# One decode step of a hybrid layer: small stores and skewed loads issued by POOL instead of SP, and copies of old cache rows placed behind weight loads

## The chip, the cores and the metric

The kernel runs on one core of one Trainium2 chip. The metric is the device time of one execution in microseconds; every kernel is run several times and the median is taken. TensorE is called PE in the profile, VectorE DVE, ScalarE ACT, GpSimd POOL and SyncE SP. SP computes nothing here: it only issues transfers, in order. POOL does both, it computes and issues, also in order.

## The reference, cut to what matters

One step of a layer for two groups of tokens with the same weights: 512 prompt tokens of one sequence and 64 sample tokens (8 sequences of 8), with a width of 1024. The input is scaled and shifted by a vector that depends on the sequence, then projected once; two branches (chunkwise retention with 4 heads, and dilated window attention in 3 groups with a relative bias) are gated, added and projected, and a second block gathers rows of an expert table.

```python
def _ada(c, w_ada, b_ada):
    mod = jax.nn.silu(c) @ w_ada + b_ada
    return jnp.split(mod[:, None, :], 6, axis=-1)
...
    def step(s, inp):
        qc, kc, vc = inp
        scores = jnp.einsum('bihd,bjhd->bhij', qc, kc) * intra
        o = jnp.einsum('bhij,bjhe->bihe', scores, vc)
        o = o + jnp.einsum('bihd,bhde->bihe', qc, s) * q_dec
        s = s * chunk_dec + jnp.einsum('bjhd,bjhe->bhde', kc * k_dec, vc)
        return s, o
```

Part of the output are the new retention states of both groups and the new caches of the attention. For the sample group a new cache is the old one without its oldest rows and with the 8 new ones, so most of it is a copy of old rows from one place in HBM to another.

## The kernel before

**Weights.** All weights stream through in units of 128 x 1024 numbers (512 KB), in a fixed order. `load_units` (L392) has SP load a unit into one of 3 raw buffers (`wraw`; 4 more serve in the first part of the kernel). ACT makes the upper half of its digits (`whi`, L315), DVE the rest (`wlo`, L316), and PE multiplies three times (`mm3`, L423 to L425). Later units that feed the experts are split by ACT (L1433) and POOL (L1434). SP issues a load when the raw buffer is free, that is, when `wlo` of the unit three earlier is done.

**What else SP issues.** Besides the weights nearly everything: constants, rows of old caches, outputs. The places of this change are five:
- L491: `ada_half` works out a quarter of a modulation vector (`m`), PE spreads it over 9 rows, and the 9 x 256 result (`m9`, one buffer) is stored into `modD` in HBM. 16 times, from 247 to 582 us.
- L525: the bias vectors of the attention are made in pieces (`vt`, two buffers) and stored into `vecD` in HBM. 6 times.
- L531: `skewed` loads `vecD` once and writes it many times, one row for each query position, into another tensor in HBM: `skp` 1024 rows for the prompt, `sks` 64 rows for the sample. 3 of each. What reads them later (L650, L1213) stays on SP.
- L711: `retention_s` stores the new state of a sample head, 128 x 8 x 128 numbers. 4 times.
- L936: `retention` stores the new state of a prompt head (`st`), 128 x 128 numbers. 4 times.

**Copies of old rows.** `copy_old(n, ins)` takes the next n of 104 copies and has SP issue them behind the instruction `ins`:

```python
    def copy_old(n, ins):
        with tc.issue_after(ins):
            for _ in range(n):
                p = next(old, None)
                if p:
                    SP.dma_start(*p)
```

`CR = 8` of them come with each head of `retention`, 32 in all; the others come with weight loads later on and stay where they are. `CS_ = 0`, so the call at L711 issues none.

**What POOL does.** At the start it scales and shifts the transposed input of both groups (`xT`, L508 and L509, two halves). From 64 to 433 us it loads the cached keys of the sample group (`kt`, L742, 32 tiles of 588 KB, 128 rows) and finishes each tile by copying the new keys into it (L744), for which it waits until the tile has landed. Later it gathers the rows of the experts (L1111).

**What sets the order.** A scheduler sorts the instructions of each engine by a simulated timeline, and each engine then runs its list in order. So a change of the issuing engine, or of what `copy_old` is tied to, moves other rows too.

Of the kernel before, what the change touches and what calls it, by code (L numbers as in the profile page):

```python
# [29 lines left out]
NVEC = VEC_G[3]  # L30
# [29 lines left out]
CR = 8  # L60
CS_ = 0
# [163 lines left out]
def body(tc, I, O, dbg=None):  # L225
    nc = tc.nc
    PE, DVE, ACT, POOL, SP = nc.tensor, nc.vector, nc.scalar, nc.gpsimd, nc.sync
# [3 lines left out]
    def raw(ap, offset, dims):  # L231
        return bass.AP(tensor=ap.tensor, offset=ap.offset + offset, ap=dims)
# [62 lines left out]
# [6 lines that stand above are left out]
# [69 lines left out]
    raws, units, state = [], [], {"done": 0, "bank": ac_ps, "ada": None}  # L370
# [38 lines left out]
    def take(name, c, u, n=2):  # L409

        a = state["done"]
        while len(units) < len(order) and sum(not plain(i) for i in range(a, len(units))) < UB:
            load_units()
            if len(units) == len(raws):
                break
            split_unit()
        load_units()
        assert order[a:a + n] == [(name, c, u + i) for i in range(n)] and len(units) >= a + n, (order[a], name, c, u)
        state["done"] += n
        return units[a:a + n]  # L420
# [42 lines left out]
    modD = DR.tile([9, 4096], F32, name="modD")  # L463
    xT = A.tile([128, 8, NS + L], F32, name="xT")

    def ada_half(pl, c, half):

        w = take("w_ada", c, 2 * half)
        ps = sp_ps()
        for z in range(2):  # L470
            for q in range(4):
                PE.matmul(ps[32 * q:32 * q + 32, 0:256], cst[:, 4 * z + q, :], *both(w, 4 * z + q), start=z == 0, stop=z == 1)
        m = pl.tile([106, 256], F32, name="m19", tag="m19", bufs=3)
        o = 512 * c + 256 * half
        SP.dma_start(m[105:106, :], I["b_ada"][:, o:o + 256])
        ACT.activation(m[0:105, :], ps[0:105, 0:256], AF.Copy)
        pt = tr_ps()
        if c < 4:
            for b in range(2):
                PE.matmul(pt[:, 128 * b:128 * b + 65], m[:, 128 * b:128 * b + 128], sel19[:, 0:65], start=True, stop=True)  # L480
            v = pt[:, 0:256].rearrange("p (b c) -> p b c", b=2)[:, :, 0:65]
            b = 4 * (c % 2) + 2 * half
            if c < 2:
                DVE.tensor_copy(shT[:, b:b + 2, :], v)
            else:
                DVE.tensor_scalar(scT[:, b:b + 2, :], v, 1.0, None, op0=OP.add)
        else:
            PE.matmul(pt[0:9, 0:256], sel19[:, 65:74], m, start=True, stop=True)
            t = pl.tile([9, 256], F32, name="m9", tag="m9", bufs=1)
            DVE.tensor_copy(t, pt[0:9, 0:256])  # L490
            SP.dma_start(modD[:, o - 2048:o - 1792], t)  # L491

    hh, hl = wide("xh"), wide("xl")
    h = lambda k, s=slice(None): (hh[:, k, s], hl[:, k, s])
# [18 lines left out]
    vecD = DR.tile([8, NVEC], F32, name="vecD")  # L513
# [4 lines left out]
    for g in range(NG):  # L518
        for o in range(VEC_G[g], VEC_G[g + 1], 512):
            e = min(o + 512, VEC_G[g + 1])  # L520
            ps = ac_ps()
            PE.matmul(ps[0:8, :e - o], rel[:, 8 * g:8 * g + 8], oh[:, o:e], start=True, stop=True)
            t = A.tile([8, 512], F32, name="vt", tag="vt", bufs=2)
            DVE.tensor_copy(t[:, :e - o], ps[0:8, :e - o])
            SP.dma_start(vecD[:, o:e], t[:, :e - o])  # L525
    A.release()

    def skewed(name, off, n, rows):

        t = DR.tile([8, rows, n], F32, name=name)  # L530
        SP.dma_start(t, raw(vecD, off, [[NVEC, 8], [0, rows], [1, n]]))  # L531
        return lambda h0, h, r, first, w, step=1: raw(t, h0 * rows * n + first, [[n - step, r], [rows * n, h], [1, w]])

    def skewed_p(g):
# [133 lines left out]
    def retention_s(hp):  # L668
        qks = RS.tile([64, 512], F32, name="qks", tag="qks", bufs=1)
        for half in range(2):  # L670
            proj_s(RS, qks[:, 256 * half:256 * half + 256], hs, take("w_rqk_s", hp, 2 * half))
        q4 = qks.rearrange("p (n m z d) -> p n m z d", n=2, m=2, z=2)
        rs4 = rope_s.rearrange("p i n (z d) -> p i n z d", z=2)
        for n in range(2):
            for z in range(2):
                DVE.tensor_tensor(r1[:, n, :, z], q4[:, n, :, z], rs4[:, 0, n, z, None, :].to_broadcast([64, 2, 64]), op=OP.mult)
                POOL.tensor_tensor(r2[:, n, :, z], q4[:, n, :, 1 - z], rs4[:, 1, n, z, None, :].to_broadcast([64, 2, 64]), op=OP.mult)
        DVE.tensor_tensor(r1, r1, r2, op=OP.add)
        rot = r1.rearrange("p n m z d -> p (n m z d)")
        qkT = RS.tile([128, 4, 64], F32, name="qkT", tag="qkT", bufs=1)  # L680
        transpose64(qkT, rot, 4)
        ons = sp_ps()
        for j in range(2):
            hd = 2 * hp + j
            hcol = slice(128 * hd, 128 * hd + 128)
            diag = raw(qm, 0, [list(qm.ap[0]), [NB * TS + TS, NB], [1, TS]])
            bt = lambda a: a.rearrange("p (b t) -> p b t", b=NB)
            DVE.tensor_tensor(diag, bt(qkT[:, j, :]), bt(qdec_s[:, hd, :]), op=OP.mult)
            psc = tr_ps()
            PE.matmul(psc[0:64, 0:64], qkT[:, 2 + j, :], qkT[:, j, :], start=True, stop=True)  # L690
            sc = RS.tile([64, 64], F32, name="scs", tag="scs", bufs=2)
            DVE.tensor_tensor(sc, psc[0:64, 0:64], intra_s[:, hd, :], op=OP.mult)
            s0 = RS.tile([128, NB, 128], F32, name="s0", tag="s0", bufs=2)
            with tc.issue_after(state["load"]):
                SP.dma_start(s0, I["state"][hd])
            vb = vbs[j]
            o = ons[0:64, 128 * j:128 * j + 128]
            PE.matmul(o, sc, rvs[:, hcol], start=True, stop=False)
            for b in range(NB):
                PE.matmul(o, qm[:, b].rearrange("p b t -> p (b t)"), s0[:, b, :], start=False, stop=b == NB - 1)  # L700
            POOL.tensor_tensor(vb, rvs[:, None, hcol].to_broadcast([64, NB, 128]),
                               bmask[:, :, None].to_broadcast([64, NB, 128]), op=OP.mult)
            kds = RS.tile([64, 128], F32, name="kds", tag="kds", bufs=2)
            DVE.tensor_scalar(kds, rot[:, 256 + 128 * j:384 + 128 * j], kdec_s[:, hd:hd + 1], None, op0=OP.mult)
            dec = float(np.exp(np.float32(LG[hd] * np.float32(TS))))
            for q in range(2):
                pn = tr_ps()
                PE.matmul(pn, kds, vb[:, 4 * q:4 * q + 4, :], start=True, stop=True)
                s4 = s0[:, 4 * q:4 * q + 4, :]
                DVE.scalar_tensor_tensor(s4, s4, dec, pn.rearrange("p (b e) -> p b e", b=4), op0=OP.mult, op1=OP.add)  # L710
            copy_old(CS_, SP.dma_start(O["st_s"][0, :, hd].rearrange("b d e -> d b e"), s0).ins)  # L711
        y = head_norm(RS, ons[0:64, 0:256].rearrange("p (c e) -> p c e", c=2), 2)
        DVE.tensor_tensor(y[:, 0:2, :], y[:, 0:2, :], rgs[:, 256 * hp:256 * hp + 256].rearrange("p (c e) -> p c e", c=2), op=OP.mult)
        pt = tr_ps()
        for j in range(2):
            PE.transpose(pt[:, 64 * j:64 * j + 64], y[:, j, :], ident[0:64, 0:64])
        stack64(ras[:, 2 * hp:2 * hp + 2, :], pt[:, 0:128].rearrange("p (j t) -> p j t", j=2))
# [192 lines left out]
    def retention(hp):  # L910
        for j in range(2):
            hd = 2 * hp + j
# [18 lines left out]
            st = R.tile([128, 4, 128], F32, name="st", tag="st", bufs=2)  # L931
            dec = float(np.exp(np.float32(LG[hd] * np.float32(128))))
            DVE.tensor_copy(st[:, 0, :], pst[:, 0:128])
            for c in range(1, 4):
                DVE.scalar_tensor_tensor(st[:, c, :], st[:, c - 1, :], dec, pst[:, 128 * c:128 * c + 128], op0=OP.mult, op1=OP.add)
            copy_old(CR, SP.dma_start(O["st_p"][0, 0, hd], st[:, 3, :]).ins)  # L936
            po = ac_ps()
            for c in range(4):
                s = slice(128 * c, 128 * c + 128)
# [25 lines left out]
    G2, t = s4k("G2s"), s4k("l1s")  # L965
# [4 lines left out]
    B2, t = s4k("B2s"), s4k("l1bs")  # L970
# [183 lines left out]
    t = T.tile([8, 4, 128], F32, name="sel8", tag="st8", bufs=2)  # L1154
# [46 lines left out]
    for g in range(NG):  # L1201
# [8 lines left out]
        for hf in range(2):  # L1210
            n = 256 if g == 0 else 128
# [83 lines left out]
    for z, s in enumerate((NM[0], LS[0])):  # L1295
# [3 lines left out]
        t = T.tile([8, 512], F32, name="st8", tag="st8", bufs=2)  # L1299
# [28 lines left out]
    for p in range(4):  # L1328
        for g in range(NG):
# [5 lines left out]
            else:  # L1335
                t = T.tile([128, 512], F32, name="mt", tag="lg", bufs=LGB)
# [55 lines left out]
    for c, ts in ((0, (0, 1, 2, 3)), (1, (0, 1, 2, 3)), (2, (0,)), (3, (0,)), (2, (1,)), (3, (1,)), (2, (2, 3)), (3, (2, 3))):  # L1392
# [6 lines left out]
        for t in ts:  # L1399
# [13 lines left out]
            for kq in range(2):  # L1413
# [4 lines left out]
                o = (slice(None), slice(0, 4), tiles[t])  # L1418
# [237 lines left out]
```

## Time and profile before

| | |
|---|---|
| median of 3 runs | 2457.9 us (2453.2 to 2463.07) |
| profiled execution, its own time | 2460.05 us |
| span of the profiled execution | 2458.3 us |
| busy share of the span | PE 91%, DVE 71%, ACT 41%, POOL 46% |
| granted clock of PE, mean | 0.95 |
| transfers | 677.54 MB, mean 276 GB/s |
| queue that SP's and ACT's direct transfers use, q1 | 439.54 MB, 51.7% of 16 engines' span |
| POOL's queue, q0 | 221.67 MB, 25.3% |

The span is the time from the first to the last instruction that the profiler saw on the core; the time of the execution holds a little more. An engine's share counts the time in which it works on an instruction; waits and issues of transfers don't count.

### The profile page before, as it was taken

To read this page: it belongs to the slowest core of one execution; us is meant where nothing else is said; L and a number is where in the kernel's file an instruction comes from. 1 tells how busy PE (TensorE), PEld (TensorE's weight loads), DVE (VectorE), ACT (ScalarE), POOL (GpSimd) and SP (SyncE) were. 2 spreads that over 40 slices of the span, in tenths; PEclk is the share of its full clock that TensorE was granted. 3 is DMA by queue.
4 is the path that set the end of the run, shared out by engine and by line. 5 is a ranking of instruction groups with operands and counts; after the bars stand their busy time and mean duration, and the time that the engine had idled before them with its cause. 6 is when DMAs were issued, how large, how long until landed. Compare 5 with 4: busy or idle time off the path is not lost.

```text
span 2458.3 us, 35746 instructions
## 1 busy us (share of the span) xinstructions
PE 2238.2 (91%) x12729; PEld 1882.9 (77%) x12729; DVE 1734.0 (71%) x3069; ACT 1010.1 (41%) x1663; POOL 1137.6 (46%) x946
## 2 busy tenths in 40 slices
PE   7789999968789997899889999889999999999994
PEld 4776566656677875899879999878887888888784
DVE  4464121254678778779999992488888887888887
ACT  2461222234455553233358886333333333333332
POOL 1022010033125644423556654676666667666773
PEclk8899999988899997999989999999999999999997
DMA  8785876566798997386768778788999998999882
GB/s 297 257 285 202 304 276 203 168 201 222 237 322 284 331 354 286 134 292 228 279 200 298 276 262 281 243 292 314 330 337 340 321 337 321 319 339 347 326 307 73
DMA packets 226703, 677.54 MB, mean 276 GB/s; under 512 B 27804, under 2 KB 84764, under 8 KB 223036
## 3 DMA queue, kind: packets, MB, share of 16 engines
q1 hardware_dynamic: 157392, 439.54, 51.7%
q0 software_dynamic: 60224, 221.67, 25.3%
q10 hardware_dynamic: 8908, 14.06, 1.6%
q8 instruction: 100, 1.64, 0.3%
q14 instruction: 79, 0.64, 0.1%
HBM read 617.40 MB, written 115.55 MB: 298 GB/s over the span
## 4 chain that ended last, share of the span: by engine, by line
PE 43%; DVE 19%; DMA 8%; issue 4%; ACT 3%; POOL 1%; ACTq 0%; SPq 0%; POOLq 0%; DVEq 0%
PE mm L423 6%; PE mm L425 6%; PE mm L424 5%; PE tr L425 4%; PE tr L423 4%; PE tr L424 3%; PE ac L425 3%; PE ac L423 3%; PE ac L424 3%; DVE wlo L316 2%; DVE ys L1129 2%; DMA act<-act 2%; DVE oh L1510 2%; DMA wraw<-in_w_q_s_dram 1%; PE ac L1511 1%
## 5 line engine op out<-in xcount | busy, mean ns | idle before, releaser
L316 DVE TENSOR_TENSOR wlo<-wraw,whi 128x1024 fp32r<-128x1024 f32 x304 | 389.2, 1285 | 326.1 <-ACT whi L315 302.4
L315 ACT ACTIVATE whi<-wraw 128x1024 fp32r<-128x1024 f32 x304 | 319.7, 1057 | 441.2 <-PE mm L424 174.3
L1434 POOL TENSOR_TENSOR wlo<-wraw,whi 128x1024 fp32r<-128x1024 f32 x128 | 321.3, 2513 | 144.6 <-ACT whi L1433 142.0
L423 PE MATMUL tr<-x,whi 128*128 128x384 f32 x1024 | 350.5, 342 | 28.2 <-ACT whi L1433 14.2
L425 PE MATMUL tr<-x,wlo 128*128 128x384 f32 x1024 | 348.5, 340 | 2.5 <-POOL wlo L1434 2.5
L424 PE MATMUL tr<-x,whi 128*128 128x384 f32 x1024 | 348.6, 340 | 0.0
L1111 POOL DMA_INDIRECT row<-in_v_dram,e x192 | 241.6, 1258 | 169.5 <-DVE y L1129 69.9
L1111 POOL DMA_INDIRECT row<-in_u_dram,e x192 | 239.1, 1246 | 158.6 <-DVE row L1120 124.8
L423 PEld LDWEIGHTS tr<-x,whi 128*128 128x128 f32 x1024 | 194.5, 190 | 37.6 <-ACT whi L1433 19.3
L425 PEld LDWEIGHTS tr<-x,wlo 128*128 128x128 f32 x1024 | 194.3, 190 | 4.3 <-POOL wlo L1434 3.1
L424 PEld LDWEIGHTS tr<-x,whi 128*128 128x128 f32 x1024 | 194.4, 190 | 1.8
L1129 DVE SCALAR_TENSOR_TENSOR y<-row,acts,y 128x1024 f32<-128x1024 f32 x127 | 189.8, 1495 | 8.4 <-DMA row<-in_v_dram,e 7.5
L1433 ACT ACTIVATE whi<-wraw 128x1024 fp32r<-128x1024 f32 x128 | 135.0, 1055 | 127.9 <-DMA wraw<-in_uT_dram 36.3
L1120 DVE SCALAR_TENSOR_TENSOR row<-row,h2g 128x1024 f32<-128x1024 f32 x128 | 177.4, 1403 | 10.8 <-DMA row<-in_u_dram,e 10.8
L423 PE MATMUL mm<-xh,whi 128*128 128x512 f32 x384 | 155.3, 404 | 0.1
L425 PE MATMUL mm<-xh,wlo 128*128 128x512 f32 x384 | 153.9, 401 | 0.0
L424 PE MATMUL mm<-xl,whi 128*128 128x512 f32 x384 | 153.6, 400 | 0.0
L424 PE MATMUL ac<-wlo,wh 128*128 128x512 f32 x384 | 152.3, 397 | 0.0
L423 PE MATMUL ac<-whi,wh 128*128 128x512 f32 x384 | 150.4, 398 | 0.0
L423 PE MATMUL mm<-whi,xh 128*128 128x256 f32 x448 | 132.6, 298 | 10.9 <-DVE gr L1359 3.3
L425 PE MATMUL ac<-whi,wl 128*128 128x512 f32 x384 | 139.8, 396 | 0.0
L1439 ACT ACTIVATE act<-tr 128x384 f32<-128x384 f32 x128 | 61.9, 484 | 183.0 <-PE tr L425 179.7
(412 smaller groups left out, 5336.3 us busy)
## 6 DMA issues: line engine op xcount, KB each, us to landing
wraw<-in_uT_dram SPq DMA_DIRECT2D x128, 512.0 KB
wraw<-in_v_dram SPq DMA_DIRECT2D x128, 512.0 KB
out_dram<-in_cache_dram SPq DMA_DIRECT2D x64, 508.0 KB
wraw<-in_w_ada_dram SPq DMA_DIRECT2D x48, 512.0 KB
act<-act SPq DMA_DIRECT2D x128, 192.0 KB
gate<-stage SPq DMA_DIRECT2D x12, 2048.0 KB
gt<-gate SPq DMA_DIRECT2D x191, 128.0 KB
kt<-in_kc_dram POOLq DMA_DIRECT2D x32, 588.0 KB
```

The source lines that it names most:

```text
L315: ACT.activation(hi, src, AF.Copy)
L316: return DVE.tensor_tensor(lo, src, fv(hi), op=OP.subtract).ins
L423: PE.matmul(ps, a[0], b[0], start=first, stop=False)
L424: PE.matmul(ps, a[0], b[1], start=False, stop=False)
L425: PE.matmul(ps, a[1], b[0], start=False, stop=last)
L1111: POOL.indirect_dma_start(out=r, out_offset=None, in_=I[table], in_offset=bass.IndirectOffsetOnAxis(ap=e[:, j:j + 1], axis=0))
L1120: DVE.scalar_tensor_tensor(u, u, 1.0, h2, op0=OP.mult, op1=OP.mult, accum_out=a[:, j:j + 1])
L1129: DVE.scalar_tensor_tensor(y, v, a[:, j:j + 1], y, op0=OP.mult, op1=OP.add)
L1433: ACT.activation(uh, u, AF.Copy)
L1434: POOL.tensor_tensor(ul, u, fv(uh), op=OP.subtract)
L1439: ACT.activation(a, ps[:, 0:ND], AF.Gelu)
L1510: E.tensor_scalar(oh0[:, j, :], num, col(0), col(2), op0=OP.is_equal, op1=OP.mult)
```

## The change

Four kinds of stores and the skewed loads are issued by POOL: 36 issues leave SP. The copies of old rows that came with the state of a prompt head are tied to the weight load that was issued last when `retention` is written (`state["load"]`) instead of the state's store. `retention` handles two heads at a time, so two sets of 8 copies come behind one load.

```diff
--- before.py
+++ after.py
@@ -488,7 +488,7 @@
             PE.matmul(pt[0:9, 0:256], sel19[:, 65:74], m, start=True, stop=True)
             t = pl.tile([9, 256], F32, name="m9", tag="m9", bufs=1)
             DVE.tensor_copy(t, pt[0:9, 0:256])
-            SP.dma_start(modD[:, o - 2048:o - 1792], t)
+            POOL.dma_start(modD[:, o - 2048:o - 1792], t)
 
     hh, hl = wide("xh"), wide("xl")
     h = lambda k, s=slice(None): (hh[:, k, s], hl[:, k, s])
@@ -522,13 +522,13 @@
             PE.matmul(ps[0:8, :e - o], rel[:, 8 * g:8 * g + 8], oh[:, o:e], start=True, stop=True)
             t = A.tile([8, 512], F32, name="vt", tag="vt", bufs=2)
             DVE.tensor_copy(t[:, :e - o], ps[0:8, :e - o])
-            SP.dma_start(vecD[:, o:e], t[:, :e - o])
+            POOL.dma_start(vecD[:, o:e], t[:, :e - o])
     A.release()
 
     def skewed(name, off, n, rows):
 
         t = DR.tile([8, rows, n], F32, name=name)
-        SP.dma_start(t, raw(vecD, off, [[NVEC, 8], [0, rows], [1, n]]))
+        POOL.dma_start(t, raw(vecD, off, [[NVEC, 8], [0, rows], [1, n]]))
         return lambda h0, h, r, first, w, step=1: raw(t, h0 * rows * n + first, [[n - step, r], [rows * n, h], [1, w]])
 
     def skewed_p(g):
@@ -708,7 +708,7 @@
                 PE.matmul(pn, kds, vb[:, 4 * q:4 * q + 4, :], start=True, stop=True)
                 s4 = s0[:, 4 * q:4 * q + 4, :]
                 DVE.scalar_tensor_tensor(s4, s4, dec, pn.rearrange("p (b e) -> p b e", b=4), op0=OP.mult, op1=OP.add)
-            copy_old(CS_, SP.dma_start(O["st_s"][0, :, hd].rearrange("b d e -> d b e"), s0).ins)
+            POOL.dma_start(O["st_s"][0, :, hd].rearrange("b d e -> d b e"), s0)
         y = head_norm(RS, ons[0:64, 0:256].rearrange("p (c e) -> p c e", c=2), 2)
         DVE.tensor_tensor(y[:, 0:2, :], y[:, 0:2, :], rgs[:, 256 * hp:256 * hp + 256].rearrange("p (c e) -> p c e", c=2), op=OP.mult)
         pt = tr_ps()
@@ -933,7 +933,8 @@
             DVE.tensor_copy(st[:, 0, :], pst[:, 0:128])
             for c in range(1, 4):
                 DVE.scalar_tensor_tensor(st[:, c, :], st[:, c - 1, :], dec, pst[:, 128 * c:128 * c + 128], op0=OP.mult, op1=OP.add)
-            copy_old(CR, SP.dma_start(O["st_p"][0, 0, hd], st[:, 3, :]).ins)
+            POOL.dma_start(O["st_p"][0, 0, hd], st[:, 3, :])
+            copy_old(CR, state["load"])
             po = ac_ps()
             for c in range(4):
                 s = slice(128 * c, 128 * c + 128)
```

After L936 the changed kernel has one line more, so its L1156 is L1155 of before.

What the scheduler makes of it shows at three places. A row is the line, the operation, what is written and read, and the shape; x2 means two such rows in a row.

The first place is the start, 38 to 85 us in the trace of before. SP before, with the vectors' stores (`vecD<-vt`) and the skewed loads (`skp`, `sks`) between the weights:

```order
35 L531 DMA skp_355<-vecD 1024x1x383
36 L525 DMA vecD<-vt 8x270
37 L525 DMA vecD<-vt 8x512
38 L392 DMA wraw<-in_w_av_dram 128x1024
39 L531 DMA skp_4197<-vecD 1024x1x255
40 L392 DMA wraw<-in_w_aqk_s_dram 128x1024 x2
41 L392 DMA wraw<-in_w_rvg_dram 128x1024
42 L392 DMA wraw<-in_w_aqk_s_dram 128x1024 x2
43 L531 DMA sks_357<-vecD 64x1x527
44 L531 DMA skp_4199<-vecD 1024x1x255
45 L525 DMA vecD<-vt 8x512
46 L525 DMA vecD<-vt 8x206
```

The same place on SP after:

```order
31 L392 DMA wraw<-in_w_av_dram 128x1024 x2
32 L475 DMA m_296<-in_b_ada_dram 1x256
33 L392 DMA wraw<-in_w_av_dram 128x1024
34 L392 DMA wraw<-in_w_aqk_s_dram 128x1024 x2
35 L392 DMA wraw<-in_w_rvg_dram 128x1024
36 L392 DMA wraw<-in_w_aqk_s_dram 128x1024 x2
37 L392 DMA wraw<-in_w_rvg_dram 128x1024
38 L392 DMA wraw<-in_w_aqk_s_dram 128x1024 x3
```

And POOL there after; before, it has only the four rows of L508 and L509 here, then the product of L701:

```order
9 L508 TENSOR_TENSOR xT<-xT,scT 128x4x64
10 L525 DMA vecD<-vt 8x383
11 L525 DMA vecD<-vt 8x512
12 L509 TENSOR_TENSOR xT<-xT,shT 128x4x64
13 L531 DMA skp_355<-vecD 1024x1x383
14 L531 DMA skp_4197<-vecD 1024x1x255
15 L525 DMA vecD<-vt 8x270
16 L525 DMA vecD<-vt 8x512
17 L508 TENSOR_TENSOR xT<-xT,scT 128x4x64
18 L509 TENSOR_TENSOR xT<-xT,shT 128x4x64
19 L531 DMA sks_357<-vecD 64x1x527
20 L525 DMA vecD<-vt 8x512
```

The twelve stores and skewed loads have left the weights' queue; on POOL two large skewed loads and four stores now stand ahead of the second half of the scaled input.

The second place is the attention of the sample group, from 194 us on, on POOL. Before:

```order
21 L742 DMA kt<-in_kc_dram 128x1176 x2
22 L744 COPY kt<-kTs 128x3x8 x2
23 L701 TENSOR_TENSOR x_1671<-rvs,kc_bmask 64x1024
24 L742 DMA kt<-in_kc_dram 128x1176 x2
25 L744 COPY kt<-kTs 128x3x8 x2
26 L701 TENSOR_TENSOR x_1671<-rvs,kc_bmask 64x1024
27 L742 DMA kt<-in_kc_dram 128x1176 x2
28 L744 COPY kt<-kTs 128x3x8 x2
29 L742 DMA kt<-in_kc_dram 128x1176 x2
```

After:

```order
36 L742 DMA kt<-in_kc_dram 128x1176 x2
37 L711 DMA out_dram<-s_1761 128x8x128
38 L744 COPY kt<-kTs 128x3x8 x2
39 L701 TENSOR_TENSOR x_1671<-rvs,kc_bmask 64x1024
40 L742 DMA kt<-in_kc_dram 128x1176 x2
41 L711 DMA out_dram<-s_1787 128x8x128
42 L744 COPY kt<-kTs 128x3x8 x2
43 L742 DMA kt<-in_kc_dram 128x1176 x2
44 L735 COPY qz_379<-qTs 64x12x8 x4
45 L711 DMA out_dram<-s_1914 128x8x128
46 L744 COPY kt<-kTs 128x3x8 x2
47 L711 DMA out_dram<-s_1940 128x8x128
```

The states' stores (L711) now stand between a pair of `kt` loads and the copies that finish that pair; the stores of L491 follow in the same way.

The third place is the prompt's retention, 575 to 680 us in the trace of before, on SP. Before:

```order
285 L491 DMA modD<-m_4543 9x256
286 L392 DMA wraw<-in_w_q_s_dram 128x1024 x2
287 L936 DMA out_dram<-st 128x128
288 L300 DMA out_dram<-in_cache_dram 16x7680
289 L300 DMA out_dram<-in_cache_dram 16x8064 x4
290 L300 DMA out_dram<-in_cache_dram 16x8128 x3
291 L392 DMA wraw<-in_w_q_s_dram 128x1024 x6
292 L936 DMA out_dram<-st 128x128
293 L300 DMA out_dram<-in_cache_dram 16x8128 x5
294 L300 DMA out_dram<-in_cache_dram 16x7680
295 L300 DMA out_dram<-in_cache_dram 16x8064 x2
296 L392 DMA wraw<-in_w_q_s_dram 128x1024 x6
```

After:

```order
250 L392 DMA wraw<-in_w_q_s_dram 128x1024 x2
251 L300 DMA out_dram<-in_cache_dram 16x7680
252 L300 DMA out_dram<-in_cache_dram 16x8064 x4
253 L300 DMA out_dram<-in_cache_dram 16x8128 x8
254 L300 DMA out_dram<-in_cache_dram 16x7680
255 L300 DMA out_dram<-in_cache_dram 16x8064 x2
256 L392 DMA wraw<-in_w_q_s_dram 128x1024 x14
257 L392 DMA wraw<-in_w_av_dram 128x1024 x5
258 L300 DMA out_dram<-in_cache_dram 16x8064 x2
259 L300 DMA out_dram<-in_cache_dram 16x8128 x8
260 L300 DMA out_dram<-in_cache_dram 16x7680
261 L300 DMA out_dram<-in_cache_dram 16x8064 x4
```

The four sets of 8 copies have become two of 16, the first ahead of 14 units of w_q_s, the second behind the fifth unit of w_av, and no state's store stands ahead of them.

## Rows read from the trace of the kernel before

**Rows 1.** The page: busy time, share of the span, instructions of each engine.
```profile
PE 2238.2 (91%) x12729; PEld 1882.9 (77%) x12729; DVE 1734.0 (71%) x3069; ACT 1010.1 (41%) x1663; POOL 1137.6 (46%) x946
```

**Rows 2.** Engine busy times by stretch, then granted clock, transfer engines' busy share, GB/s.
```profile
40.00:60.00 20.00, 16.08 (x118) 13.96 (x117) 13.15 (x20) 9.21 (x15) 3.31 (x3) 0.92 0.76 218
60.00:80.00 20.00, 12.04 (x77) 11.05 (x78) 6.93 (x8) 6.39 (x10) 5.71 (x6) 0.77 0.77 245
80.00:100.00 20.00, 16.13 (x116) 15.52 (x116) 5.74 (x7) 6.42 (x11) 0.00 (x0) 0.89 0.70 231
246.00:492.00 246.00, 239.92 (x1404) 152.74 (x1402) 47.52 (x69) 62.68 (x104) 20.44 (x53) 0.97 0.69 238
570.00:600.00 30.00, 30.00 (x146) 23.57 (x145) 14.08 (x28) 10.58 (x15) 8.90 (x7) 0.96 0.52 158
600.00:660.00 60.00, 45.09 (x265) 38.72 (x264) 37.16 (x86) 29.33 (x43) 14.36 (x13) 0.83 0.83 273
660.00:700.00 40.00, 35.92 (x288) 34.01 (x286) 34.98 (x130) 18.29 (x33) 5.65 (x4) 1.00 0.66 219
700.00:740.00 40.00, 36.52 (x238) 31.51 (x240) 23.09 (x54) 19.76 (x45) 10.61 (x10) 0.91 0.97 346
```

**Rows 3.** TensorE's waits to 123 us: waited for, us in total, times, longest.
```profile
PE ac L560 <- ACT whi L315: 11.1, 4, 4.4
...
PE ac L560 <- DVE vt L524: 2.2, 1, 2.2
```

**Rows 4.** ScalarE's waits, 25 to 100 us, columns as above.
```profile
ACT whi L315 <- DMA wraw<-in_w_aqk_s_dram: 14.0, 3, 7.5
```

**Rows 5.** Waits of SP's queue, 25 to 100 us, columns as above.
```profile
SPq L525 <- DVE wlo L316: 7.7, 2, 4.2
...
SPq L525 <- DMA skp<-vecD: 6.1, 1, 6.1
SPq L392 <- DMA skp<-vecD: 4.9, 1, 4.9
```

**Rows 6.** Chain that ended last, 590 to 740 us: start, us, what.
```profile
600.34 1.24 DVE wlo L316
601.60 12.39 DMA wraw<-in_w_q_s_dram
...
648.02 4.37 DMA wraw<-in_w_av_dram
...
679.79 12.70 DMA wraw<-in_w_av_dram
```

**Rows 7.** Timeline of SP's queue: start, us, line, transfer, count.
```profile
581.55 0.36 SPq L392 DMA_DIRECT2D wraw<-in_w_q_s_dram  x1
...
595.77 5.43 SPq L300 DMA_DIRECT2D out_dram<-in_cache_dram  x8
```

**Rows 8.** Waits of SP's queue, 570 to 720 us.
```profile
SPq L936 <- DVE st L935: 14.1, 3, 9.3
```

**Rows 9.** POOL's kt loads, grouped by line: durations in ns, min/median/max.
```profile
L742 POOL DMA_DIRECT2D kt<-in_kc_dram x32: 530/530/1047, 64.4 to 433.5; - x32
```

**Rows 10.** The page's groups: POOL's gathers, busy us, mean ns, idle before.
```profile
L1111 POOL DMA_INDIRECT row<-in_v_dram,e x192 | 241.6, 1258 | 169.5 <-DVE y L1129 69.9
```

**Rows 11.** Timeline of POOL: start, us, line, product, idle before.
```profile
34.22 0.98 POOL L509 TENSOR_TENSOR xT<-xT,shT 128x256 f32<-128x256 f32 x1 [14.14 <-DVE shT L484]
...
48.63 0.98 POOL L509 TENSOR_TENSOR xT<-xT,shT 128x256 f32<-128x256 f32 x1 [7.04 <-DVE shT L484]
...
168.23 1.73 POOL L744 COPY kt<-kTs 128x24 f32<-128x24 f32 x2 [102.52 <-ACT kTs L623]
```

**Rows 12.** Waits of SP's queue, 180 to 492 us.
```profile
SPq L491 <- DVE m L490: 16.9, 5, 8.2
```

**Rows 13.** POOL's waits, 200 to 500 us.
```profile
POOL kt L742 <- PE ac L748: 111.6, 13, 18.6
POOL kt L744 <- DMA kt<-in_kc_dram: 75.3, 26, 6.5
```

## The prediction

> **What bounds the kernel now.** I read the page first. TensorE is busy 91% of the span, VectorE 71% [rows 1], and the transfer engines reach 97% and 346 GB/s only from 700 to 740 us [rows 2]. So no one of them bounds the whole. From 246 to 492 us TensorE has 239.9 us of work in 246: almost nothing can be won there, but whatever makes it wait there is lost in full. From 40 to 100 us it is idle for 3.92 + 7.96 + 3.87 = 15.8 us, and from 600 to 740 for 14.9 + 4.1 + 3.5 = 22.5 us. After 740 the program's order is nearly the same in both kernels, so I take that part as moved, not changed. What the change can win lies in those two idle pieces, some 38 us together.
>
> Then I asked who is waited for in each.
>
> Early piece: TensorE's waits before 123 us name the split weights (11.1 us in 4 waits) and once a vector's buffer (vt, 2.2 us) [rows 3]. ScalarE, which makes the first half of the split, waits in its turn for weight units on their way: 14.0 us in 3 waits for w_aqk_s [rows 4]. And SP, which issues those units in order, stands before a vector's store 7.7 + 6.1 us and before a weight load behind a skewed load 4.9 us: 18.7 us in all [rows 5]. The 16 transfer engines are busy 0.76, 0.77 and 0.70 there [rows 2], so 15.4 us of 60 are free.
>
> Late piece: the chain there is a string of weight units in flight: five pieces from 601.60 (12.39 us) to 648.02 (4.37 us), then 12.70 us for a w_av unit [rows 6]. The SP timeline says why: after each retention head's state store come 8 copies of old cache rows, and the weights queue behind them. Just ahead of it, 570 to 600, the engines are only 52% busy at 158 GB/s while TensorE is full [rows 2]; the first 8 copies come at 595.77 [rows 7], because they are placed behind a store that waits for the state (14.1 us in 3 waits) [rows 8].
>
> **Part 1: stores of vectors and skewed loads (L525, L531) to POOL.** SP loses 12 issues; the weights behind them no longer wait for vt, for a landed vecD or for a skewed load. TensorE's waits to be won are 11.1 + 2.2 = 13.3 us. The bytes stay: the three large skewed loads, 1024 rows of 255, 255 and 383 numbers, are 3.66 MB, 10.6 us at the 346 GB/s of [rows 2], and they still share the engines with the weights; but 15.4 us are free there, so I take two thirds, **9 us**. Bounds: 0 (the units land no sooner) and 13.3.
>
> POOL's price for a skewed load is not in the trace: no POOL transfer there has 1024 rows. The nearest rows: a kt load of 128 rows takes POOL 0.53 us [rows 9] and a gather of 128 rows 1.26 us [rows 10]; eight times as many rows make 4.2 and 10 us, both estimates. I take 4.2, since the kt load is a plain transfer like these and the gather is not; with 0.53, should the rows not count, the part is worth the same. What is queued behind: the second scaled input (L508) and its shift (L509, at 48.63) [rows 11] now stand behind two skewed loads and two stores. They could start at 35.2, where the first L509 ends, + 2 x 4.2 + about 2 for the stores = 46 us, and end about 49 instead of 49.6: nothing is late. With 10 they end near 59, and TensorE's products on them move by some 9 us, while the weights run ahead; Part 1 is then worth about 1 us. After that POOL has little to do until 168 us [rows 11], so the rest costs nothing.
>
> The Trainium skill, "DMA: Bandwidth & Descriptors", section "Issuing engines are not separate DMA queues", speaks against this part: transfers issued by several engines run on the same 16 engines, and only the issuing time is saved, usually a small thing. By that rule Part 1 would be near 0 and the time near 2451; no run here shows yet whether it holds, but the trace has SP stand for 18.7 us, which is more than issuing.
>
> **Part 2: modulation and state stores (L491, L711) to POOL.** 16 and 4 issues leave SP, where those of the modulations wait 16.9 us for m between 180 and 492 [rows 12]. SP was ahead there (TensorE is full), so the gain is nothing. POOL takes 16 x 0.53 = 8 us for the modulations and 4 x 4.2 us for the states (1024 rows of 512 B), and the waits come with them, in front of kt loads and of the copies that finish a kt tile. These copies wait for kt to land in any case, 75.3 us over 26 waits, 2.9 us each [rows 13]: a state store of 4.2 us makes them about 1.3 us late, four times, 5 us. POOL stands idle 111.6 us in 13 waits, 8.6 us each, before it may load a next kt [rows 13], and most of what is late comes out of that slack. I take **+1 us**. Bounds: 0, and the 39 us of the first rival below.
>
> **Part 3: state stores of the prompt (L936) to POOL, copies tied to a weight load.** Four stores cost POOL 0.5 us each, beside other work. What counts is where the 32 copies go: two bursts of 16. The first now stands behind the second w_q_s load, issued at 581.55 [rows 7], some 4 us sooner without the two modulation stores ahead of it, and no longer waits for a state. From 577 to 600 the engines have about 0.48 x 23 = 11 us free, 3.8 MB at 346 GB/s, or 7 copies of 16 x 8128 numbers (0.52 MB, 1.5 us each). The other 9 (13.5 us) collide with the third w_q_s unit, which lands near 609 where its split could begin near 604.7, some 4.4 us behind the split that begins at 600.34 [rows 6]: 4 us of TensorE's 14.9 us of idle time from 600 to 660 stay, **11 go**. From then on 14 w_q_s units come without a copy between them, where before 16 copies (24 us) came. The second burst stands behind the fifth w_av load. 16 copies are 24 us; the three raw buffers hold three units, at 22 units in 100 us 4.5 us each, 13.6 us: the next w_av units come some 10 us late. Before, a 12.70-us wait for a w_av unit there [rows 6] went with 4.1 us of idle TensorE from 660 to 700 [rows 2], since retention's other products fill in; I take +5. The copies of before at 674 and 698 us no longer stand ahead of w_aqk and of the attention, where TensorE is idle 3.5 us from 700 to 740: -2. Sum: -11 + 5 - 2 = **-8 us**. Bounds: -22 (all idle time from 600 to 740 goes) and +9 (the fill wins nothing, as w_q_s units land behind 16 copies instead of 8, and the stall costs 10). VectorE sets a floor for hopes beyond: it is busy 35.0 of 40 us from 660 to 700 [rows 2].
>
> **Sum.** -9 + 1 - 8 = -16 us against the profiled execution's own 2460.05 us, that is 2444; the median of the runs, 2457.9, lies 2.15 lower, so I predict **2442 us**.
>
> **Rivals.**
> *Slower: POOL's order becomes the wait.* POOL executes in order, and from 195 to 433 it loads and finishes kt for an attention in which TensorE has 2.5% of idle time. If a state store holds POOL for 10 us, kt copies are 10 - 2.9 = 7.1 us late four times, 28 us; if the modulations bring SP's 16.9 us of waiting for m along, together 45, of which the 6 us that TensorE is idle from 246 to 492 hide: 39. Part 1 is then worth 1, and the sum is 39 - 1 - 8 = +30: 2488 us. It decides from 21 us in the middle on. For it: POOL's waits for kt, ended only by its landing. Against: POOL sat idle 111.6 us before kt loads (L742), so there is room, and m is made by VectorE, which is 19% busy there [rows 2]. Chance 0.10.
> *No change: weights gain nothing from an earlier place.* The same bytes on the same engines; in the early piece the skewed loads now go out at once and share with the weights (0), and in the late one the second burst's 10 us stall takes back what the fill wins (-11 + 10 = -1). Time 2457. For it: the fullest stretch, 700 to 740, has 0.97 of the engines busy. Against: 0.70 to 0.77 early, and 0.52 before 600. The rule of the Trainium skill named above is this rival's first half. Chance 0.25.
> *Only one of the two pieces is won* (9 or 8): some 2449. With a little more from the piece that is won, it lies on the bound between faster and same. Chance 0.20.
> *Both pieces won outright*, 13.3 + 22 = 35: 2423. Against: VectorE's load, the second burst. Chance 0.10.
>
> **How the numbers follow.** The forecast has 0.35. A measurement of this kernel can tell some 0.5% (12.3 us) from no change: faster below 2445.6, slower above 2470.2. Faster: forecast and both pieces, 0.45, and two fifths of "one piece", 0.08: 0.53. Same: 0.25 and the rest of that case, less 0.01 for the ends of "no change" that lie higher: 0.36. Slower: 0.10 + 0.01 = 0.11. The range goes from 2420, just below both pieces outright, to 2462, no change with some loss in the middle; it leaves out the slower rival and the ends of the others.
>
> **What the next profile would show.** Part 1: SP's waits before L392 from 25 to 100 without vecD or skewed tiles, ScalarE's 14.0 us for weights gone down to a third, POOL's skewed loads of some 4 us each, and the scaled input ended before 50 us. Part 2: TensorE still 97% busy from its 246 to 492; if kt copies start over 5 us after kt has landed and TensorE waits for them, the slower rival holds. Part 3: copies starting some 18 us sooner, transfers over 80% busy in the 20 us before the w_q_s products, TensorE idle under 5 us in the 60 us after, and a wait of about 10 us for a w_av unit behind the second burst. The prediction is wrong if a POOL issue takes 10 us or more, if TensorE is idle in the kt stretch, or if w_q_s units land later behind 16 copies than they did behind 8.

## The result, and the profile after

The changed kernel takes 2439.64 us (median of 6 runs, 2432.32 to 2444.91), the kernel before on the same chip 2457.2 us (6 runs, 2453.2 to 2463.07): a ratio of 0.9923, 95% interval 0.9907 to 0.9939, or 19 us less (15 to 23). On another chip the ratio was 0.9945 (0.9924 to 0.9966). The profiled execution took 2440.74 us, its span is 2439.0.

The page's first part, as [rows 1]:

```profile
PE 2229.5 (91%) x12729; PEld 1885.9 (77%) x12729; DVE 1726.5 (71%) x3069; ACT 1008.4 (41%) x1663; POOL 1170.1 (48%) x982
```

Busy times by stretch of the changed kernel, with the columns of [rows 2]:

```profile
40.00:60.00 20.00, 11.26 (x68) 9.26 (x68) 8.39 (x12) 5.63 (x9) 1.99 (x3) 0.67 1.02 261
60.00:80.00 20.00, 18.83 (x143) 17.72 (x143) 12.56 (x16) 9.67 (x16) 6.53 (x6) 0.97 0.52 165
80.00:100.00 20.00, 14.27 (x92) 13.49 (x92) 4.75 (x6) 5.05 (x9) 3.68 (x6) 0.83 0.74 246
...
570.00:600.00 30.00, 30.00 (x151) 24.01 (x150) 13.99 (x31) 10.13 (x15) 14.70 (x14) 1.00 0.94 318
600.00:660.00 60.00, 53.87 (x369) 48.74 (x368) 36.74 (x81) 31.66 (x48) 12.51 (x12) 0.91 0.79 260
660.00:700.00 40.00, 31.42 (x198) 28.41 (x197) 35.91 (x133) 17.58 (x30) 4.33 (x5) 0.74 0.55 181
700.00:740.00 40.00, 38.94 (x252) 32.34 (x251) 25.44 (x56) 21.14 (x48) 13.28 (x10) 1.00 0.77 280
```

From 40 to 60 us TensorE lost 4.8 us of work against [rows 2] (11.26 for 16.08), with the transfer engines now full (1.02 busy, at 261 GB/s), and it caught up after 60. From 600 to 740 its idle time is 6.1 + 8.6 + 1.1 = 15.8 us for 22.5. Between 570 and 600 the transfers run at 0.94 for 0.52.

What stands on POOL at the start, by the timeline, with the idle time before it in brackets:

```profile
34.95 2.23 POOL L531 DMA_DIRECT2D skp<-vecD  x2
39.20 1.13 POOL L525 DMA_DIRECT2D vecD<-vt  x2 [2.02 <-DVE vt L524]
...
57.53 0.98 POOL L509 TENSOR_TENSOR xT<-xT,shT 128x256 f32<-128x256 f32 x1 [16.14 <-DVE shT L484]
...
212.79 0.94 POOL L711 DMA_DIRECT2D out_dram<-s  x1
```

Two skewed loads of 1024 rows cost POOL 2.23 us together, a state store 0.94. The second L509 did not wait behind them: it waited 16.14 us for its input, the shift, and came at 57.53 for 48.63 in [rows 11]. The timeline of ScalarE says why:

```profile
53.96 1.06 ACT L315 ACTIVATE whi<-wraw 128x1024 fp32r<-128x1024 f32 x1 [11.65 <-DMA wraw<-in_w_av_dram]
54.92 0.37 ACT L476 ACTIVATE m<-sp 105x256 f32<-105x256 f32 x1
```

A w_av unit that SP had issued before 40 us is awaited for 11.65 us, and the next modulation row (`m`, L476), from which the shift is made, stands behind it in ScalarE's order.

SP at the prompt's retention, as [rows 7], and what it waited for there, as [rows 8]:

```profile
569.77 4.29 SPq L392 DMA_DIRECT2D wraw<-in_w_q_s_dram  x2
574.11 16.28 SPq L300 DMA_DIRECT2D out_dram<-in_cache_dram  x16
591.89 38.26 SPq L392 DMA_DIRECT2D wraw<-in_w_q_s_dram  x14
631.67 10.94 SPq L392 DMA_DIRECT2D wraw<-in_w_av_dram  x5
642.66 19.14 SPq L300 DMA_DIRECT2D out_dram<-in_cache_dram  x16
662.70 3.98 SPq L392 DMA_DIRECT2D wraw<-in_w_av_dram  x3
```

```profile
SPq L392 <- DMA wraw<-in_w_av_dram: 9.6, 2, 8.7
```

The first 16 copies are issued 21.7 us sooner than the first 8 were, and a wait of SP of 8.7 us for a w_av unit stands behind the second burst. POOL's waits in the attention, as [rows 13]:

```profile
POOL kt L744 <- DMA kt<-in_kc_dram: 63.3, 26, 6.9
POOL kt L742 <- PE ac L748: 51.1, 8, 12.7
POOL modD L491 <- DVE m L490: 43.9, 10, 9.8
```

POOL waits for kt 63.3 us for 75.3, before it may load kt 51.1 for 111.6; the 43.9 us for `m` fit into that slack.

### The profile page after: what moved, and what is told of

Read it like the earlier page. It is cut to its first block, busy times and chain, and to the rows that moved or that the text cites. A ratio compares the mean times of both kernels' runs of the same rounds, so it can differ in the third digit from the quotient of the medians.

```text
span 2439.0 us, 35771 instructions
## 1 busy us (share of the span) xinstructions
PE 2229.5 (91%) x12729; PEld 1885.9 (77%) x12729; DVE 1726.5 (71%) x3069; ACT 1008.4 (41%) x1663; POOL 1170.1 (48%) x982
## 4 chain that ended last, share of the span: by engine, by line
PE 34%; DVE 23%; DMA 10%; issue 6%; POOL 3%; ACT 2%; SPq 0%; POOLq 0%; DVEq 0%; ACTq 0%
PE mm L423 4%; PE mm L425 4%; PE mm L424 4%; PE tr L425 3%; PE tr L423 3%; PE tr L424 3%; DVE wlo L316 2%; DVE ys L1130 2%; PE ac L425 2%; PE ac L424 2%; PE ac L423 2%; DMA act<-act 2%; DMA row<-in_u_dram,e 2%; DVE oh L1511 2%; DMA row<-in_v_dram,e 1%
## 5 line engine op out<-in xcount | busy, mean ns | idle before, releaser
L316 DVE TENSOR_TENSOR wlo<-wraw,whi 128x1024 fp32r<-128x1024 f32 x304 | 396.7, 1311 | 310.7 <-ACT whi L315 291.2
L1435 POOL TENSOR_TENSOR wlo<-wraw,whi 128x1024 fp32r<-128x1024 f32 x128 | 326.3, 2551 | 140.6 <-ACT whi L1434 131.1
L1130 DVE SCALAR_TENSOR_TENSOR y<-row,acts,y 128x1024 f32<-128x1024 f32 x127 | 184.0, 1449 | 10.9 <-DMA row<-in_v_dram,e 9.7
L315 ACT ACTIVATE wh<-wt 128x384 fp32r<-128x384 f32 x128 | 66.1, 523 | 181.7 <-DVE wt L1578 180.8
```

Source lines behind the costliest of these rows:

```text
L315: ACT.activation(hi, src, AF.Copy)
L316: return DVE.tensor_tensor(lo, src, fv(hi), op=OP.subtract).ins
L1130: DVE.scalar_tensor_tensor(y, v, a[:, j:j + 1], y, op0=OP.mult, op1=OP.add)
L1435: POOL.tensor_tensor(ul, u, fv(uh), op=OP.subtract)
```

## The experiments

**One part alone.** Three kernels have one part of the change each: p1_vectors_skewed the lines L525 and L531, p2_mods_states L491 and L711, p3_copies L936. A fourth, p23_no_vectors, has the last two:

```diff
-            POOL.dma_start(vecD[:, o:e], t[:, :e - o])
+            SP.dma_start(vecD[:, o:e], t[:, :e - o])
...
-        POOL.dma_start(t, raw(vecD, off, [[NVEC, 8], [0, rows], [1, n]]))
+        SP.dma_start(t, raw(vecD, off, [[NVEC, 8], [0, rows], [1, n]]))
```

> The kernel before with only the vectors' stores and the skewed loads (L525, L531) moved to POOL. Theory now, from the two traces: the first two skewed loads are issued together near 35 us and hold the transfer engines until about 58 us, a w_av unit lands some 10 us late, ScalarE's next modulation row stands behind it in ScalarE's order, and the sample input is late by 9 us; the weights that were issued meanwhile give it back by 200 us. So 0, between 2453 and 2461 us, TensorE without an instruction for some 6 us near 50 us, and instructions near 220 us within 2 us of where they were. Rival (as I predicted): 9 us less, near 2448, with instructions near 220 us some 9 us earlier.

> The kernel before with only the modulations' and the sample states' stores (L491, L711) moved to POOL. Theory now: SP no longer stands before these stores, weights come earlier, and from 200 to 560 us some 6 us are won, as the two traces show (instructions there come 1 us later at 220 and 5.3 us earlier at 560): near 2451 us. Rival (as I predicted): nothing is won there, and the 6 us belong to a higher granted clock that the early part's different pauses brought: 2457 +- 2, instructions at 560 us within 2 us of where they were.

> The kernel before with only the change at L936: the prompt states' stores on POOL and the copies tied to a weight load. Theory: as predicted, the first 16 copies fill the engines before 600 us, TensorE's idle time from 600 to 660 falls by some 9 to 11 us, 4 to 5 come back behind the second burst, and 4 to 8 us remain by 840 us: 2449 to 2453. Rival: most of the change's 17 us comes from here, 2440 to 2444, because what follows 840 us also runs better with it (another 10 us between 840 and 2300). Other rival: 0.

> The changed kernel with the vectors' stores and skewed loads back on SP. Theory: these are worth nothing, so this is as fast as the changed kernel, 2437 to 2443 us, or up to 2 us faster. Rival (as I predicted): it is 9 us slower than the changed kernel, near 2449.

Measured on one chip, against 27 runs of before (median 2460.24 us):

| kernel | median us | ratio (95% interval) |
|---|---|---|
| p1_vectors_skewed | 2460.57 | 0.9989 (0.9972 to 1.0007) |
| p2_mods_states | 2445.6 | 0.9943 (0.9923 to 0.9962) |
| p3_copies | 2450.01 | 0.9957 (0.9938 to 0.9977) |
| p23_no_vectors | 2434.29 | 0.9883 (0.9857 to 0.9908) |

Part 1 is worth nothing that these runs resolve, Part 2 some 14 us and Part 3 some 11; the two together 29, more than the whole change's 19, though the two intervals meet (0.9908 and 0.9907). The profile of p1_vectors_skewed repeats the early loss; busy times and ScalarE's waits:

```profile
40.00:60.00 20.00, 13.57 (x81) 11.82 (x81) 10.06 (x15) 6.16 (x10) 2.30 (x4) 0.67 1.02 265
60.00:80.00 20.00, 17.81 (x136) 16.66 (x135) 11.99 (x12) 9.82 (x15) 6.51 (x6) 0.98 0.56 179
```

```profile
ACT whi L315 <- DMA wraw<-in_w_av_dram: 9.5, 2, 9.3
```

**What in Part 2, and what in Part 3.** p2_mods_only moves L491 alone. p3_store_on_sp leaves the state's store on SP and ties only the copies to the load:

```diff
-            copy_old(CR, SP.dma_start(O["st_p"][0, 0, hd], st[:, 3, :]).ins)
+            SP.dma_start(O["st_p"][0, 0, hd], st[:, 3, :])
+            copy_old(CR, state["load"])
```

> The kernel before with only the modulations' stores (L491) moved to POOL. Theory, from the trace with both stores of Part 2 moved: what is won is a w_ada unit that stood on SP behind a store of L491 near 250 us, a pause of TensorE of some 2 us and a half clock for the products behind it; so most of that kernel's gain (it measured 0.9943 of before) is here: 0.994 to 0.997, and no half clock from 240 to 260 us. Rival: the state stores (L711) carry it, and this is within 0.002 of before.

> The kernel before with the copies tied to a weight load, as in the change, but the prompt states' stores left on SP, behind their heads' states. Theory: the gain of Part 3 (0.9957) is the place of the copies, ahead of 600 us, so the same, 0.995 to 0.997. Rival: weights still wait on SP behind the state's store (14 us in 3 waits before), and half of it or more is lost: 0.998 to 1.000.

Measured 0.9958 (0.9942 to 0.9975) and 0.9967 (0.9946 to 0.9988). The first is within the interval of both stores together, so the state stores' share is not resolved, and the mechanism was not the one that I had expected: the pause for w_ada is still there (waits of TensorE, 235 to 300 us), and so is a part at the low clock from 240 to 260.

```profile
PE sp L472 <- DMA wraw<-in_w_ada_dram: 3.0, 1, 3.0
```

```profile
240.00:260.00 20.00, 15.19 (x129) 7.16 (x131) 8.30 (x21) 6.11 (x15) 3.19 (x7) 0.91 0.95 344
```

In p2_mods_states that wait is gone and the clock is 1.00 there; it is gone in all profiles with the state stores on POOL. So what the modulations win is something else. The pause also varies by itself: it is 2.0 us in the first profile of before and 0.4 in before_again, further down. The second run: tying the copies to the load keeps the gain of Part 3, and no share of the store's queue is resolved.

**The skewed loads later, and fewer bytes of them.** skew_after_shift has POOL issue them behind L509 (`shifted` is its instruction); skew_one_head loads one head's rows only and leaves out those of the other seven, as its expectation says.

```diff
-        POOL.dma_start(t, raw(vecD, off, [[NVEC, 8], [0, rows], [1, n]]))
+        with tc.issue_after(shifted):
+            POOL.dma_start(t, raw(vecD, off, [[NVEC, 8], [0, rows], [1, n]]))
```

```diff
-        t = DR.tile([8, rows, n], F32, name=name)
-        POOL.dma_start(t, raw(vecD, off, [[NVEC, 8], [0, rows], [1, n]]))
...
+        t = DR.tile([1, rows, n], F32, name=name)
+        POOL.dma_start(t, raw(vecD, off, [[NVEC, 1], [0, rows], [1, n]]))
...
```

> The changed kernel with the skewed loads placed on POOL behind the second shift of the sample input (L509), so that they start some 10 us later and after it. Theory: the two skewed loads issued at 35 us were what made a w_av unit land late and the input with it; now the shift ends before 50 us, instructions near 220 us come 4 to 9 us earlier than in the changed kernel, and the time is that of the changed kernel without Part 1, 0.986 to 0.990 of before. Rival: the bytes collide with other weights later and nothing is won: 0.992 as the changed kernel.

> The changed kernel, with skewed loads of one head's rows instead of eight, which all heads then read: seven eighths of the skewed bytes are left out (3.2 of 3.66 MB), and the bias is that of the first head everywhere. Theory: Part 1 won nothing because these bytes hold the transfer engines wherever they are issued; without them the w_av unit near 40 us lands as early as in the kernel before, TensorE's idle time from 40 to 123 us falls from 19.6 us to 10 or less, and instructions near 220 us come 6 to 12 us earlier than in the changed kernel. Rival: something else held the input (POOL's or ScalarE's order), and instructions near 220 us stay within 3 us.

skew_after_shift measured 0.9913 (0.9896 to 0.9929), no different from the changed kernel. The shift came at 50.98 us instead of 57.53, but by 225 us nothing is left of it: ScalarE now waits 21.6 us for w_aqk_s units, and TensorE for their results (its waits from 40 to 180 us):

```profile
ACT whi L315 <- DMA wraw<-in_w_aqk_s_dram: 21.6, 6, 8.6
```

```profile
PE tr L623 <- DVE arow L566: 10.6, 3, 9.2
```

skew_one_head measured 0.9875 (0.9847 to 0.9903), 2422.36 us. TensorE is idle 2.0 us from 40 to 100 for 15.6 in the changed kernel:

```profile
40.00:60.00 20.00, 18.91 (x141) 16.86 (x141) 15.03 (x22) 10.13 (x16) 7.58 (x13) 0.89 0.87 283
60.00:80.00 20.00, 19.36 (x156) 18.42 (x155) 10.83 (x11) 11.23 (x18) 4.27 (x3) 1.00 0.86 290
80.00:100.00 20.00, 19.78 (x160) 18.98 (x159) 15.38 (x16) 14.29 (x21) 0.00 (x0) 1.00 0.69 230
```

So the skewed data are what the early piece waits for: over the profiles of all the other runs this idle time goes from 10.8 to 17.0 us. Whichever queue issues the 3.66 MB, and when, costs the same within what these runs tell; without seven eighths of them some 19 us go (first mark below). Bytes and rows shrink together here, so which of the two costs the time is not shown. It is twice what I had priced: I took 346 GB/s for these bytes, and the engines were full at 261 GB/s.

**The second burst spread out.** p23_spread is p23_no_vectors with the second 16 copies placed singly behind 16 loads:

```diff
-            copy_old(CR, state["load"])
+            if hp == 0:
+                copy_old(CR, state["load"])
...
+            if 4 <= i - order.index(("w_q_s", 0, 0)) < 20:
+                copy_old(1, ins)
```

> The changed kernel without Part 1, and the second 16 copies placed one behind each of 16 weight loads (w_q_s from the fifth on, then w_av) instead of in one burst behind a w_av load. Theory: the burst cost some 5 us of TensorE's idle time from 660 to 700 us and a half clock there; without it 0.984 to 0.987 of before (the same kernel with the burst: 0.9883). Rival: the copies slow the w_q_s units that the burst left alone, and nothing is won or some 5 us lost: 0.988 to 0.991.

Measured 0.9916 (0.9886 to 0.9947), between the 0.9883 of the same kernel with the burst and the 0.9928 of its repeat below: no gain. Busy times:

```profile
600.00:660.00 60.00, 49.67 (x317) 43.09 (x316) 37.26 (x90) 29.38 (x44) 10.96 (x9) 0.86 0.90 333
660.00:700.00 40.00, 33.30 (x234) 31.22 (x233) 37.69 (x139) 19.92 (x35) 7.98 (x9) 0.88 0.23 64
```

Against the same kernel with the burst (53.18 and 53.51 us, then 30.10 and 31.18, in its two profiles) TensorE loses some 3.7 us up to 660 and gains some 2.7 behind it. The transfer engines are busy 0.23 behind 660: the copies now compete with the w_q_s units, and behind 660 the free transfer time is of no use, as VectorE is busy 37.69 of 40 us there.

**The same program again.** before_again and after_again are the two kernels once more, p23_again the one without Part 1.

> The kernel before once more, for a second profile of it. Theory: what the profiles show after 860 us, where the order of the instructions is the same in both kernels, differs from one execution to another by some 5 to 10 us, so this profile differs from the first of before by up to that at 2300 us, and by less than 3 us up to 560 us. Rival: it agrees with the first within 2 us everywhere, and the 10 us that the changed kernel wins after 860 us are its own.

> The changed kernel once more, on the same chip as the next one. Theory: Part 1 costs some 5 to 10 us where Parts 2 and 3 are in, so this is slower than the changed kernel without Part 1 by 0.002 to 0.004 of before. Rival: both are the same within 0.001, at 0.990 to 0.992, and the difference between the runs so far came from their chips.

> The changed kernel without Part 1 (vectors' stores and skewed loads on SP), on the same chip as the one before. Theory: 0.986 to 0.990, faster than the changed kernel by 5 to 10 us. Rival: as the changed kernel, 0.990 to 0.992.

after_again measured 0.9945 (0.9924 to 0.9966), p23_again 0.9928 (0.9902 to 0.9954), on one chip: 2442.9 us (2438.02 to 2444.31) and 2437.12 (2427.84 to 2442.86). On this one chip leaving out Part 1 is 5.8 us faster than the changed kernel, which lies within the two intervals. The profiled execution of before_again took 2442.95 us, 17 us less than the first profile of the same program, and the runs of before on that chip lay between 2447.15 and 2461.82: one profile of this kernel cannot carry a difference of 10 us. So I read the parts from marks in all the profiles: the start of ScalarE's second qkT (L623) and of h2s (L976; L977 in the changed kernel), from the timelines as here for the changed kernel:

```profile
226.44 0.38 ACT L623 ACTIVATE qkT<-tr 128x256 f32<-128x256 f32 x1
```

```profile
562.00 1.06 ACT L977 ACTIVATE h2s<-h2s 64x1024 f32<-64x1024 f32 x1
```

| kernel | parts in it | qkT | qkT to h2s | h2s to the end |
|---|---|---|---|---|
| before | - | 225.5 | 341.3 | 1891.5 |
| before_again | - | 221.4 | 338.5 | 1881.3 |
| p1_vectors_skewed | 1 | 226.6 | 344.3 | 1888.3 |
| p2_mods_states | 2 | 228.2 | 335.1 | 1882.0 |
| p2_mods_only | half of 2 | 227.0 | 337.4 | 1890.2 |
| p3_copies | 3 | 225.3 | 346.3 | 1875.4 |
| p3_store_on_sp | 3 but the store | 222.4 | 340.8 | 1883.0 |
| changed kernel | 1, 2, 3 | 226.4 | 335.6 | 1877.0 |
| after_again | 1, 2, 3 | 224.9 | 332.3 | 1883.8 |
| skew_after_shift | 1, 2, 3 | 226.0 | 337.1 | 1881.6 |
| p23_no_vectors | 2, 3 | 221.7 | 332.6 | 1878.8 |
| p23_again | 2, 3 | 226.7 | 335.5 | 1869.8 |
| p23_spread | 2, 3 | 223.9 | 335.9 | 1882.7 |
| skew_one_head | 1, 2, 3 | 207.0 | 333.1 | 1879.6 |

Without skew_one_head, the means are: the first mark 226.0 with Part 1 and 224.7 without; the middle 335.2 with Part 2 (all eight below 337.5) and 342.2 without (all five above 338.4); the rest 1879.0 with Part 3 and 1886.7 without, ranges that just overlap. That is +1.3, -7.0 and -7.7 us; the first is no difference, as its ranges (224.9 to 226.6 and 221.4 to 228.2) lie one within the other.

## Why the prediction was right, and where it was not

The total held: 2442 us predicted, 2439.64 measured. It held by luck in two of its three terms: -9 for Part 1 stood for about nothing and +1 for Part 2 for about -14, and the two errors cancel. The parts measured alone add up to -28 us and the whole change to -19, or some -13 on the other chip; the intervals are too wide to say that the parts take from each other.

**Part 1, -9 predicted: failed.** Measured alone -3 us (-7 to +2), by the marks +1.3. The step that failed is "15.4 us are free there, so I take two thirds". The free time lay where the skewed loads had not yet come; issued 4 and 9 us sooner, two of them at once, they fill the engines from 40 to 60 us (1.02) and a w_av unit waits among them. SP's 18.7 us of standing did go: no vecD or skewed tile is left among its waits before weight loads. But SP waited for its raw buffers instead (for wlo 23.0 us in 6 waits), as the units did not land sooner, and ScalarE's wait moved from w_aqk_s (14.0 us in [rows 4]) to w_av:

```profile
ACT whi L315 <- DMA wraw<-in_w_av_dram: 12.2, 2, 11.7
SPq L392 <- DVE wlo L316: 23.0, 6, 15.6
```

POOL's price was mis-sized (1.1 us for 1024 rows, not 4.2), which changed nothing, and the shift was late for another reason than the one I had weighed. The rule of the Trainium skill, "DMA: Bandwidth & Descriptors", section "Issuing engines are not separate DMA queues", holds for this part: 0.9989 for another issuing engine, and 19 us at the first mark for less data. Part 2 won more than its 20 issues had taken on SP (16 of 0.26 to 0.57 us and 4 of 0.40), which the rule leaves open.

**Part 2, +1 predicted: failed.** Measured -14 us (-19 to -9), by the marks -7.0 in its stretch. The step that failed is "SP was ahead there (TensorE is full), so the gain is nothing". TensorE's idle time between the marks did not fall, and its busy time shrank with the same number of products, as these windows from mark to mark show for before, the changed kernel and p2_mods_states:

```profile
225.50:566.80 341.30, 305.13 (x1784) 198.48 (x1785) 97.82 (x142) 92.81 (x151) 50.94 (x83) 0.93 0.70 232
```

```profile
226.40:562.00 335.60, 296.96 (x1784) 197.88 (x1784) 97.28 (x142) 92.28 (x152) 61.09 (x98) 0.94 0.71 238
```

```profile
228.20:563.30 335.10, 293.39 (x1784) 193.34 (x1784) 97.31 (x142) 92.39 (x151) 61.93 (x98) 0.96 0.71 238
```

Idle are 36.2, 38.6 and 41.7 us; 305.13 us for 1784 products became 296.96 and 293.39; the granted clock is 0.93, 0.94 and 0.96. A busy share of 97% was no proof that nothing could be won. In these profiles a part is the pause of 2 us for w_ada, behind which products ran at the low one of the two clock levels (0.87 from 240 to 260 us, 1.00 in the changed kernel). But the clock varies by itself: between the marks it is 0.93 in the first profile of before and 0.95 in before_again; with the modulations alone the pause stays, and that profile still has 337.4 between the marks, where those without Part 2 have 338.5 to 346.3. With the stores on POOL the scheduler also places kt's products (L748) later, among those of w_ada (L472); TensorE in before, then in p2_mods_states:

```profile
244.43 1.21 PE L472 MATMUL sp<-wraw,cst 128*32 128x256 f32 x13
245.48 4.13 PE L748 MATMUL ac<-kt,qz 128*32 128x136 f32 x20
```

```profile
249.24 2.26 PE L748 MATMUL ac<-kt,qz 128*32 128x136 f32 x11
251.21 0.42 PE L472 MATMUL sp<-wraw,cst 128*32 128x256 f32 x3
251.33 0.29 PE L748 MATMUL ac<-kt,qz 128*32 128x144 f32 x1
```

This share repeats: if each product counts only by what it adds to the busy time behind those started before it, L748 and L472 make 68.7 to 69.9 us of it between the marks in all eight profiles with Part 2 and 72.3 to 74.1 in all five without, some 3.7 of the 7.0 us. That the order makes them, and not SP's freedom, was not tried apart and stays open, as do the rest of the 7.0 and what Part 2 wins beyond this stretch. The slower rival did not come: a state store costs POOL 0.92 us, not 10, and nothing in TensorE's waits from 200 to 480 us names kt.

**Part 3, -8 predicted: right in size, and its pieces only in part.** Measured -11 us (-15 to -6), by the marks -7.7. In the changed kernel's windows the pieces seem to stand: 600 to 660 us 8.8 us less idle (predicted 11), 660 to 700 4.5 more (5), 700 to 740 2.4 less (2). But with Part 3 alone, in p3_copies, it is 5.1 less, 1.2 more and 0.6 less:

```profile
600.00:660.00 60.00, 50.22 (x307) 43.73 (x306) 39.70 (x96) 30.82 (x45) 17.21 (x15) 0.91 0.77 246
660.00:700.00 40.00, 34.72 (x274) 33.03 (x273) 36.44 (x142) 18.38 (x32) 4.08 (x6) 0.94 0.89 299
700.00:740.00 40.00, 37.16 (x238) 30.80 (x237) 23.88 (x50) 21.67 (x58) 12.86 (x13) 0.85 0.81 281
```

There the stores of L491 still stand ahead of the first copies, which SP issues at 586.53 instead of 574.11 (h2s at 571.64 instead of 562.00); so a part of the 8.8 us needs Part 2 as well. And the 4.5 us have another cause than the late w_av unit of my sum. SP's 8.7 us held SP: from 655 to 700 us no wait of ScalarE ends with a weight unit's landing, and TensorE waits for the prompt's activations, which VectorE reorders (`perm`) and ScalarE copies (`xh`, `xl`; TensorE's and ScalarE's waits from 570 to 740 us):

```profile
PE mm L423 <- ACT xh L1092: 5.8, 5, 1.6
PE mm L425 <- ACT xl L1092: 2.7, 4, 1.1
ACT xh L1092 <- DVE perm L1091: 5.3, 5, 1.4
ACT xl L1092 <- DVE perm L1091: 4.8, 5, 1.7
```

TensorE's two waits are 8.5 of the 8.6 us of idle time (8.8 and 8.9 us in after_again and p23_again), with VectorE busy 35.91 of 40. So the 5 came out by luck; what the second burst itself costs TensorE no run shows. The low clock there (0.74 from 660 to 700) was not in my sum; the products there took longer for it. That the copies need not wait for the state's store, p3_store_on_sp shows. Counted from h2s to the split of the same later weight unit (ScalarE's at 862.83 us in before), the eight profiles with Part 3 take 292.7 us on average (289.0 to 298.1) and the five without 296.0 (294.5 to 298.6): some 3 of the 7.7 us by then. The others come later; what makes them stays open.

## What to carry to other kernels

When a wait on an issuing queue ends with a transfer, ask whether the bytes or the queue's order held it: moving the issue to another engine helped with the second alone here, and brought the bytes forward into something else. Put bulk copies that nothing waits for just ahead of a stretch that needs bandwidth, where the table by stretches shows it free. An engine that is 97% busy can still have several per cent in its busy time. And when a predicted stall shows up at the predicted size, read who waited for what before calling it the predicted one. Profile the unchanged program twice before a stretch is read for a few us.

## What the runs showed of the hardware

A plain transfer of 1024 rows held POOL for 1.09 to 1.14 us and one of 64 rows for 0.59 to 0.65, where a kt load of 128 long rows takes 0.53: far less than in proportion to the rows. The six vectors' stores, 6.6 to 16.4 KB each, landed between 2.5 and 26.6 us after their issue (median 10.0), from 27 to 72 us, where the skewed loads were under way from 35 us on:

```profile
L531 POOL DMA_DIRECT2D skp<-vecD x3: 1088/1140/1143, 35.0 to 71.1; - x3
L531 POOL DMA_DIRECT2D sks<-vecD x3: 594/597/645, 66.1 to 88.1; - x3
```

```profile
DMA to landing us min/median/max: 2.5/10.0/26.6
```

Two executions of one program differed by 17 us in their span (2458.3 and 2441.2), with all the instructions in one order.
